# Projections of keys, queries and values into pairs of PSUM banks, with the convolution over all 1024 tokens at once

## The chip, the cores and the metric

The kernel runs on one core of a Trainium2 chip. The metric is the device time of one launch in microseconds (us). TensorE does the matmuls, VectorE (DVE in the profile), ScalarE (ACT) and GpSimd (POOL) the work on elements, and SyncE's queue (SP) issues the transfers. TensorE writes its results into PSUM, which has eight banks of 512 float32 values in each of 128 partitions.

## The reference

One decoder layer on 1024 tokens of width 1024: a half-step SwiGLU network, a mixer with two branches (gated delta rule and sparse attention), and a second half-step network. What matters here is the first branch's input:

```python
proj = h @ w_in[l]
(dn_qkv, dn_z, dn_b, dn_a, c_q, c_kv, idx_k_raw, idx_w,
 gate_a, gate_b) = split_cols(proj, IN_SPLITS)
qkv = jax.nn.silu(causal_dwconv(dn_qkv, conv_w[l])).astype(jnp.float32)
dq, dk_, dvv = split_cols(qkv, (DN_QK_W, DN_QK_W, DN_V_W))
```

The convolution is causal, has four taps, and treats each of the 3072 channels by itself: eight heads of 128 channels for each of queries, keys and values, so 24 times 128 channels.

## The kernel before, in words

Activations lie with channels on the partitions and tokens along the free dimension, in two halves of 512 tokens. Every float32 product is made of three matmuls (`mm3`, lines 139 to 141): each operand is split into a high part and a low part (`split`, lines 111 and 112: ScalarE copies the high part, VectorE or GpSimd subtracts it).

The stages, with their place in the profiled execution: the first feed-forward network (to 689 us), small projections and index queries (`small_proj`, `index_queries`, to 815), index scores (`scores`, to 904), the heads' projections and convolutions (`kq_head` for keys and queries, `v_head` for values, to about 1230), the joining of the solved triangular blocks with the gates' projections (`solve_join`, to 1315), the delta rule (`delta`, to 1600), attention (`attn_head`, to 1853), the output projection (`out_proj`, matmuls into `pwo`, from 1818 on) and the second feed-forward network.

PSUM is one pool for the whole program. Each stage builds a `Banks` object over it, which gives names to banks: a tile with tag `g` takes banks 0 and 1 in turn, `u` banks 2 and 3, `t` and `d` banks 4 to 7. `gemm` projects 1024 tokens onto 128 channels: 24 matmuls for each half into one bank called `pin`. The convolution (`conv`, lines 950 to 963) then works on each half: ScalarE copies the half with the fourth tap's weight (line 957), VectorE adds the other three taps out of PSUM (line 960, 511 to 509 elements), for the second half three more instructions add the one to three tokens that reach over from the first (line 962), and ScalarE applies Silu (line 963).

The order of instructions on each engine is found by a scheduler from the order of the program, its priorities and the tiles' dependencies; a later stage's instructions may be placed among an earlier one's where their tiles are free. Lines marked with `keep_in_program_order` are not moved.

The names that the steps below touch: `n_acc` and `n_ps` are a norm's sums of squares (GpSimd, then a matmul with ones, line 204), `rs_y` its inverse root on VectorE (lines 101 to 106), `n_rb` that root spread over the partitions by matmuls (line 181). `kq` and `vT` are convolved keys and queries, and values. `pq` are index queries, `arg` the exponents of the decays (line 920), `tb` an activation of the gates (line 1161), `sp_r` a latent being normalised (line 696). In the delta rule `o` is a head's output and `pot` its transposition. In attention `pl` are logits, `ph` and `plo` split probabilities, `pp` their transposition, and `pao` their product with the values; `mh` and `ml` are the split merged branches that `out_proj` reads.

Of the kernel before, what the change touches and what calls it, by code (L numbers as in the profile page):

```python
# [10 lines left out]
F32 = mybir.dt.float32  # L11
# [46 lines left out]
class Banks:  # L58
# [5 lines left out]
    def tile(self, shape, dtype, name, tag):  # L64
# [2 lines left out]
        self.turn[tag] += 1  # L67
        return self.pool.tile(shape, dtype, name=name, tag=f"bank{i}", bufs=1)


class Layer:
    def __init__(self, ctx, tc, I, out):
        self.ctx, self.tc, self.nc, self.I, self.out = ctx, tc, tc.nc, I, out
        self.pinned = False
        nc = self.nc
        self.const = self.pool(ctx, "const", 1)
        self.dram = ctx.enter_context(tc.tile_pool(name="dram", bufs=1, space=DRAM))
        self.stat = self.pool(ctx, "stat", 2)
        self.wp = self.pool(ctx, "w", 1)
        self.psum = self.pool(ctx, "psum", 1, space=PSUM)  # L80
        self.ident = self.const.tile([P, P], F32, name="ident")
        make_identity(nc, self.ident)
        self.ones = self.const.tile([P, P], F32, name="ones")
        nc.vector.memset(self.ones, 1.0)
# [83 lines left out]
    def pair(self, j, h):  # L168
        return self.part(j, h, 0), self.part(j, h, 1)
# [549 lines left out]
    def index_queries(self, tmp, ps, cqr, fill):  # L719

        nc = self.nc
        wh, wl = self.weights([self.I["w_iq"][0].rearrange("(k p) f -> p k f", p=P)], 2, 512)
        qs = tmp.tile([P, NB_IDX, 768], F32R, name="qs")
        for t0, n in ((256, 256), (512, 512)):
            for c in range(4):
                pq = ps.tile([P, 512], F32, name="pq", tag="g" if c % 2 else "u")
                for k in range(2):
                    self.mm3(pq[:, 0:n], wh[:, k, ts(c, P)], wl[:, k, ts(c, P)], cqr[0][:, k, t0:t0 + n],
                             cqr[1][:, k, t0:t0 + n], k == 0, k == 1)
                o = slice(t0 - 256, t0 - 256 + n)  # L730
# [205 lines left out]
        w = self.I["w_in"][0].rearrange("(k p) f -> p k f", p=P)  # L936
        return self.weights([w[:, :, c:c + m] for c, m in zip(cols, widths)], NK, sum(widths), self.splitter)

    def gemm(self, ps, weights, tags, halves=range(2)):

        wh, wl = weights
        n = wh.shape[-1]
        out = []
        for h in halves:
            pp = ps.tile([P, 512], F32, name="pin", tag=tags[h])
            for k in range(NK):
                self.mm3(pp[0:n], wh[:, k, :], wl[:, k, :], self.hhi[k][h], self.hlo[k][h], k == 0, k == NK - 1)
            out.append(pp)
        return out

    def conv(self, p, tile_i, pps, dest):

        nc = self.nc
        cw = self.cw.rearrange("p (j c) -> p c j", j=4)[:, tile_i, :]
        for h in range(2):
            y = p.tile([P, 512], F32, name="cv_y", tag="cv_y", bufs=3)
            nc.scalar.activation(y, pps[h], AF.Copy, scale=cw[:, 3:4])
            for j in (2, 1, 0):
                n = 3 - j
                nc.vector.scalar_tensor_tensor(y[:, n:512], pps[h][:, 0:512 - n], cw[:, j:j + 1], y[:, n:512], ALU.mult, ALU.add)  # L960
                if h:
                    nc.vector.scalar_tensor_tensor(y[:, 0:n], pps[0][:, 512 - n:512], cw[:, j:j + 1], y[:, 0:n], ALU.mult, ALU.add)
            nc.scalar.activation(dest(h), y, AF.Silu)

    def kq_head(self, hd, p, ps, picks):
        nc = self.nc
        kq = p.tile([P, 2, S], F32, name="kq", tag="kq", bufs=1)
        pk = self.gemm(ps, self.columns((1024 + hd * P,)), "gu")
        self.conv(p, 8 + hd, pk, lambda h: kq[:, 0, ts(h, 512)])
        pq = self.gemm(ps, self.columns((hd * P,)), "gu")  # L970
        picks(2)
        self.conv(p, hd, pq, lambda h: kq[:, 1, ts(h, 512)])

        ss = self.stat.tile([P, 2, NT], F32, name="ss")
        kts = []
        for h in range(2):
            for i in range(2):
                pt = ps.tile([P, 512], F32, name="pt", tag="t")
                for t in range(4):
                    nc.tensor.transpose(pt[:, ts(t, P)], kq[:, i, ts(4 * h + t, P)], self.ident)  # L980
                j = p.tile([P, 512], F32, name="qk_j", tag="qk_j", bufs=1)
# [28 lines left out]
        for h in range(2):  # L1010
            pg = ps.tile([P, 4, P], F32, name="pgram", tag="t")
            for t in range(4):
                for i in range(2):
                    c = 8 * h + 2 * t + i
# [17 lines left out]
    def v_head(self, hd, p, ps):  # L1032

        nc = self.nc
        pv = self.gemm(ps, self.columns((2048 + hd * P,)), "gu")
        vT = p.tile([P, S], F32, name="vT", tag="vT", bufs=1)
        self.conv(p, 16 + hd, pv, lambda h: vT[:, ts(h, 512)])
        for h in range(2):
            pt = ps.tile([P, 4, P], F32, name="pt", tag="t")
            for t in range(4):  # L1040
                nc.tensor.transpose(pt[:, t, :], vT[:, ts(4 * h + t, P)], self.ident)
            vb = p.tile([P, 4, P], F32, name="vb", tag="vb", bufs=2)
            nc.vector.tensor_mul(vb, pt, self.beta[:, hd, ts(h, 4), None].to_broadcast([P, 4, P]))
            nc.sync.dma_start(self.vbd[ts(h, 4), :, hd, :].rearrange("t p d -> p t d"), vb)
# [435 lines left out]
    def run(self):  # L1480
        nc, tc, I = self.nc, self.tc, self.I
# [8 lines left out]
        hs = ExitStack()  # L1490
        self.open_parts(hs, "hT", 0, NK, "right")
        with ExitStack() as c:
            ps = Banks(self.psum, s=(0, 1, 2, 3, 4, 5), m=(6, 7))
            self.open_x(c)
            np_ = self.pool(c, "norm1", 1)
            self.open_parts(c, "rest1", NK, 14)
# [31 lines left out]
            self.down_last(I["ffn1_wd"], 2 * NS, np_, ps, keep_x, to_mix)  # L1528
        merged, ms = self.mixer(hs)
        with ExitStack() as c:  # L1530
            ps = Banks(self.psum, s=(0, 1, 2, 3, 4, 5), m=(6, 7))
            self.open_x(c)
            self.new_x(load=True)
            np_ = self.pool(c, "norm2", 1)
# [29 lines left out]
    def mixer(self, hs):  # L1564

        nc = self.nc
        ms = ExitStack()
        with ExitStack() as km:
            keep = self.pool(km, "keep", 1)
            self.masks(keep)  # L1570
            with ExitStack() as ss:
                ps = Banks(self.psum, g=(0, 1), u=(2, 3), t=(4, 5, 6, 7), d=(4, 5, 6, 7))
                gpool = self.pool(ss, "gates", 1)
                gates = self.gates(gpool)
                self.gate_ps, self.splitter = ps, "gpsimd"
# [26 lines left out]
                with ExitStack() as c2:  # L1602
                    sp = self.pool(c2, "blocks", 1)
                    blocks = [self.solve_blocks(k, sp, ps) for k in range(2)]
                    with ExitStack() as c3:
                        p = self.pool(c3, "qkv", 1)
# [23 lines left out]
                    fill(2)  # L1630
                    fill(2)
                self.delta_state(keep)
                ps = Banks(self.psum, g=(0,), u=(2,), pq=(4, 5), pv=(1, 3), pn=(6, 7), po=(1, 3), qk=(0, 2))
                self.gate_ps, self.splitter = ps, "vector"
                dpool = self.pool(ss, "delta", 1)
                first = self.attn_first((gpool, "tz", 2), ps)
# [9 lines left out]
                for _ in first:  # L1646
                    pass
            with ExitStack() as c:
                ps = Banks(self.psum, qk=(0, 1), lg=(2, 4, 5), pt=(6, 7), ao=(3,))
                p = self.pool(c, "attn", 1)  # L1650
                mlp = self.pool(c, "merged_raw", 1)
                raw = [mlp.tile([P, S], F32, name=f"mr{k}", tag=f"mr{k}") for k in range(NK)]
# [75 lines left out]
```

## Time and profile before

| | us |
|---|---|
| median of 3 runs (lowest, highest) | 2591.26 (2591.16, 2594.76) |
| profiled execution, its own time | 2597.29 |
| its span (first to last instruction) | 2595.6 |
| TensorE busy | 2515.3 |
| VectorE busy | 1723.2 |
| ScalarE busy | 1186.2 |
| GpSimd busy | 931.1 |

The mean granted clock of TensorE is 0.981 of full speed. All durations below come from the profiled execution, which is 6.0 us longer than the median of the runs. A row of a timeline gives the start, the duration, the engine, the line, the tiles (out<-in) and, in brackets, how long the engine idled before it and for whom. The duration of a matmul reaches into the next one, so their pace is read from the starts.

### The profile page before, as it was taken

The page shows a single profiled execution, that of the slowest core. Times are in us where ns is not written, and L with a number is a line of the kernel's source. Part 1 is how long each engine was busy: PE and PEld are TensorE (multiplying, and loading weights), DVE is VectorE, ACT ScalarE, POOL GpSimd, SP SyncE. Part 2 cuts the span into 40 slices and gives each one's busy share as a digit, 9 for nine tenths or more (in the row PEclk, how much of TensorE's full clock was granted, in tenths as well). Part 3 has the DMA queues.
Part 4 walks back from the last instruction along what each step waited for, and adds up shares of the span by engine and source line. Part 5 has one row for each costly group of instructions (what it writes and reads, how often), then busy time and mean ns, then how long its engine had stood idle before and what let it go on. Part 6 is the DMA issues. An engine that isn't in the chain of part 4 may idle for free.

```text
span 2595.6 us, 36363 instructions
## 1 busy us (share of the span) xinstructions
PE 2515.3 (97%) x12694; PEld 2068.8 (80%) x12694; DVE 1723.2 (66%) x3419; ACT 1186.2 (46%) x2314; POOL 931.1 (36%) x721
## 2 busy tenths in 40 slices
PE   7999999999999989989999999999999999999998
PEld 6788888888787778867778887998787888888886
DVE  6755566676555677899746685777667555557766
ACT  4444344333434566546258636655434444444333
POOL 1555445333434223332200002443325554554340
PEclk9999999999999989999999899999999999999999
DMA  6243345962435144544553323222541434439642
GB/s 192 91 150 132 111 142 171 325 219 86 142 87 138 57 116 124 136 111 125 139 201 99 118 94 96 82 74 76 189 132 57 142 102 146 138 128 322 226 144 74
DMA packets 364376, 352.73 MB, mean 136 GB/s; under 512 B 87128, under 2 KB 271264, under 8 KB 363168
## 3 DMA queue, kind: packets, MB, share of 16 engines
q1 hardware_dynamic: 354848, 332.05, 40.1%
q10 hardware_dynamic: 8064, 16.78, 1.8%
q0 software_dynamic: 1280, 1.57, 0.3%
q8 instruction: 100, 1.64, 0.3%
q14 instruction: 84, 0.69, 0.1%
HBM read 234.35 MB, written 115.98 MB: 135 GB/s over the span
## 4 chain that ended last, share of the span: by engine, by line
PE 50%; DVE 7%; ACT 1%; issue 1%; DMA 0%; DVEq 0%; ACTq 0%
PE pst L139 8%; PE pst L141 8%; PE pst L140 8%; PE pin L141 2%; PE pin L139 2%; PE pin L140 2%; DVE sb_p L1071 2%; PE pn L1258 1%; PE po L1267 1%; PE pv L1253 1%; DVE cv_y L960 1%; PE pq L1248 1%; PE pwo L140 1%; PE pwo L139 1%; PE pwo L141 1%; PE pp L1372 1%
## 5 line engine op out<-in xcount | busy, mean ns | idle before, releaser
L139 PE MATMUL pst<-p,w_hi 128*128 128x512 f32 x960 | 377.9, 394 | 1.4 <-ACT p L257 0.9
L141 PE MATMUL pst<-p,w_hi 128*128 128x512 f32 x960 | 376.2, 392 | 1.8 <-DVE w_hi L112 1.8
L140 PE MATMUL pst<-p,w_hi 128*128 128x512 f32 x960 | 375.6, 391 | 1.3 <-DVE p L112 1.3
L139 PE MATMUL pin<-p,w_hi 128*128 128x512 f32 (+1 forms) x848 | 342.5, 405 | 6.4 <-DVE cv_y L960 4.2
L140 PE MATMUL pin<-p,w_hi 128*128 128x512 f32 (+1 forms) x848 | 341.0, 402 | 0.5 <-DVE p L112 0.5
L141 PE MATMUL pin<-p,w_lo 128*128 128x512 f32 (+1 forms) x848 | 340.8, 402 | 0.0
L111 ACT CAST w_hi<-w_raw 128x512 fp32r<-128x512 f32 (+2 forms) x282 | 196.3, 699 | 300.9 <-PE pst L141 126.8
L112 DVE TENSOR_TENSOR w_lo<-w_raw,w_lo 128x512 fp32r<-128x512 f32 (+1 forms) x196 | 191.5, 978 | 163.7 <-ACT w_lo L111 162.2
L141 PE MATMUL pst<-p,w_lo 128*128 128x512 f32 x728 | 284.6, 391 | 0.0
L140 PE MATMUL pst<-p,w_lo 128*128 128x512 f32 x728 | 284.4, 391 | 0.0
L139 PE MATMUL pst<-p,w_lo 128*128 128x512 f32 x728 | 282.7, 393 | 0.0
L141 PEld LDWEIGHTS pst<-p,w_hi 128*128 128x128 f32 x960 | 180.8, 188 | 43.0 <-DVE w_hi L112 2.4
L139 PEld LDWEIGHTS pst<-p,w_hi 128*128 128x128 f32 x960 | 181.0, 189 | 41.5 <-ACT p L257 1.3
L140 PEld LDWEIGHTS pst<-p,w_hi 128*128 128x128 f32 x960 | 180.8, 188 | 40.8 <-DVE p L112 1.7
L111 ACT CAST w_lo<-w_raw 128x512 fp32r<-128x512 f32 (+1 forms) x196 | 113.1, 580 | 199.0 <-DMA w_raw<-in_ffn_wg_dram 83.1
L139 PEld LDWEIGHTS pin<-p,w_hi 128*128 128x128 f32 (+1 forms) x848 | 162.0, 191 | 43.3 <-DVE cv_y L960 4.5
L141 PEld LDWEIGHTS pin<-p,w_lo 128*128 128x128 f32 (+1 forms) x848 | 161.9, 191 | 37.0 <-issue 3.1
L140 PEld LDWEIGHTS pin<-p,w_hi 128*128 128x128 f32 (+1 forms) x848 | 162.1, 191 | 36.4 <-issue 2.6
L411 DVE TENSOR_TENSOR c<-c,pst 128x512 f32<-128x512 f32 x120 | 82.0, 683 | 151.8 <-PE pst L141 113.7
L112 POOL TENSOR_TENSOR w_lo<-w_raw,w_hi 128x1024 fp32r<-128x1024 f32 (+1 forms) x43 | 106.7, 2482 | 199.6 <-ACT w_hi L111 173.2
L141 PEld LDWEIGHTS pst<-p,w_lo 128*128 128x128 f32 x728 | 136.7, 188 | 30.8
L139 PEld LDWEIGHTS pst<-p,w_lo 128*128 128x128 f32 x728 | 136.7, 188 | 30.1 <-ACT c L375 0.6
(432 smaller groups left out, 5461.7 us busy)
## 6 DMA issues: line engine op xcount, KB each, us to landing
p<-mixd SPq DMA_DIRECT2D x144, 256.0 KB, 5.6
w_raw<-in_w_in_dram SPq DMA_DIRECT2D x52, 512.0 KB, 4.0
w_raw<-in_ffn_wg_dram SPq DMA_DIRECT2D x44, 512.0 KB, 3.8
w_raw<-in_ffn_wu_dram SPq DMA_DIRECT2D x44, 512.0 KB, 3.9
mixd<-t_hi SPq DMA_DIRECT2D x72, 256.0 KB, 4.4
mixd<-t SPq DMA_DIRECT2D x72, 256.0 KB, 4.0
w_raw<-in_ffn_wd_dram SPq DMA_DIRECT2D x48, 384.0 KB, 4.3
actd<-c SPq DMA_DIRECT2D x70, 256.0 KB, 2.0
```

The source lines that it names most:

```text
L111: self.nc.scalar.copy(hi, raw)
L112: self.pin((self.nc.vector if engine == "vector" else self.nc.gpsimd).tensor_sub(lo, raw, hi))
L139: mm(ps, lhsT=wh, rhs=rh, start=first, stop=False, **kw)
L140: mm(ps, lhsT=wh, rhs=rl, start=False, stop=False, **kw)
L141: mm(ps, lhsT=wl, rhs=rh, start=False, stop=last, **kw)
L411: nc.vector.tensor_add(c[i, h], c[i, h], bank["y" if m == 1 else "z"])
L960: nc.vector.scalar_tensor_tensor(y[:, n:512], pps[h][:, 0:512 - n], cw[:, j:j + 1], y[:, n:512], ALU.mult, ALU.add)
L1071: nc.vector.tensor_mul(v, T[:, 0:i, 0:i].rearrange("p j c -> p c j"), L[:, None, 0:i, i].to_broadcast([P, i, i]))
L1248: nc.tensor.matmul(pq[:, i, :], lhsT=kq[:, h, ts(c, P)], rhs=old[:, h, :], start=True, stop=True)
L1253: nc.tensor.matmul(pv[r, i, :], lhsT=X[r, h, :], rhs=vb[r, h, :], start=True, stop=True)
L1258: nc.tensor.matmul(pn[:, i, :], lhsT=kd[r, h, :], rhs=vn[r, h, :], start=True, stop=True)
L1267: nc.tensor.matmul(po[r, i, :], lhsT=at[r, h, :], rhs=vn[r, h, :], start=True, stop=True)
```

## The change

`gemm` and `index_queries` take a tile of two banks side by side, called a pair, where they took two tiles of one bank; banks 0 to 3 become two pairs. The convolution reads a pair as 1024 tokens in a row: one copy, three instructions of VectorE and one Silu. Its buffer `cv_y` holds 1024 tokens and exists twice, where there were three of 512. The one PSUM pool is replaced by a pool for each stage, opened and closed with it: one for each feed-forward network, one for the mixer up to the join, one for the delta rule, one for attention.

```diff
+    def pair(self, name, tag="w"):
+        pairs = self.names[tag]
+        i = pairs[self.turn[tag] % len(pairs)]
+        self.turn[tag] += 1
+        return self.pool.tile([P, 2, 512], F32, name=name, tag=f"pair{i}", bufs=1)
...
-        self.psum = self.pool(ctx, "psum", 1, space=PSUM)
...
             for c in range(4):
-                pq = ps.tile([P, 512], F32, name="pq", tag="g" if c % 2 else "u")
+                if c % 2 == 0:
+                    both = ps.pair("pq")
+                pq = both[:, c % 2]
...
-    def gemm(self, ps, weights, tags, halves=range(2)):
+    def gemm(self, ps, weights, tags, halves=range(2), whole=False):
...
+        both = ps.pair("pin") if "w" in ps.names else None
         for h in halves:
-            pp = ps.tile([P, 512], F32, name="pin", tag=tags[h])
+            pp = both[:, h] if both is not None else ps.tile([P, 512], F32, name="pin", tag=tags[h])
...
-        return out
+        return both.rearrange("p h t -> p (h t)") if whole else out
...
-        for h in range(2):
-            y = p.tile([P, 512], F32, name="cv_y", tag="cv_y", bufs=3)
-            nc.scalar.activation(y, pps[h], AF.Copy, scale=cw[:, 3:4])
-            for j in (2, 1, 0):
-                n = 3 - j
-                nc.vector.scalar_tensor_tensor(y[:, n:512], pps[h][:, 0:512 - n], cw[:, j:j + 1], y[:, n:512], ALU.mult, ALU.add)
-                if h:
-                    nc.vector.scalar_tensor_tensor(y[:, 0:n], pps[0][:, 512 - n:512], cw[:, j:j + 1], y[:, 0:n], ALU.mult, ALU.add)
-            nc.scalar.activation(dest(h), y, AF.Silu)
+        y = p.tile([P, S], F32, name="cv_y", tag="cv_y", bufs=2)
+        nc.scalar.activation(y, pp, AF.Copy, scale=cw[:, 3:4])
+        for j in (2, 1, 0):
+            n = 3 - j
+            nc.vector.scalar_tensor_tensor(y[:, n:S], pp[:, 0:S - n], cw[:, j:j + 1], y[:, n:S], ALU.mult, ALU.add)
+        nc.scalar.activation(dest, y, AF.Silu)
...
-            ps = Banks(self.psum, s=(0, 1, 2, 3, 4, 5), m=(6, 7))
+            ps = Banks(self.pool(c, "psum", 1, space=PSUM), s=(0, 1, 2, 3, 4, 5), m=(6, 7))
...
-                ps = Banks(self.psum, g=(0, 1), u=(2, 3), t=(4, 5, 6, 7), d=(4, 5, 6, 7))
+                pp = ExitStack()
+                ps = Banks(self.pool(pp, "psum", 1, space=PSUM), w=(0, 1), t=(4, 5, 6, 7), d=(4, 5, 6, 7))
...
-                ps = Banks(self.psum, g=(0,), u=(2,), pq=(4, 5), pv=(1, 3), pn=(6, 7), po=(1, 3), qk=(0, 2))
+                pp.close()
+                ps = Banks(self.pool(ss, "psum", 1, space=PSUM), g=(0,), u=(2,), pq=(4, 5), pv=(1, 3), pn=(6, 7), po=(1, 3), qk=(0, 2))
...
-                ps = Banks(self.psum, qk=(0, 1), lg=(2, 4, 5), pt=(6, 7), ao=(3,))
+                ps = Banks(self.pool(c, "psum", 1, space=PSUM), qk=(0, 1), lg=(2, 4, 5), pt=(6, 7), ao=(3,))
```

The scheduler moves instructions in consequence. First, TensorE between the first network and the mixer: `n_ps` and `n_rb` belong to the norm of the second half of the tokens, `p0_00` to `p7_01` are the first half's activations (high and low), `p0_10` and on the second half's. Before:

```order
L139 MATMUL pin_6169<-p7_00_5535,w_hi_6165 128x512
L140 MATMUL pin_6169<-p7_01_5536,w_hi_6165 128x512
L141 MATMUL pin_6169<-p7_00_5535,w_lo_6166 128x512
L181 MATMUL n_rb_5806<-ident_69,rs_y_5793 128x128 x4
L139 MATMUL pin_5923<-p0_10_5509,w_hi_5894 88x512
L139 MATMUL pin_6134<-p0_10_5509,w_hi_6105 128x512
L140 MATMUL pin_5923<-p0_11_5510,w_hi_5894 88x512
L141 MATMUL pin_5923<-p0_10_5509,w_lo_5895 88x512
```

and with the change:

```order
L210 MATMUL n_ps_5782<-ones_71,n_acc_5612 128x1
L210 MATMUL n_ps_5782<-ones_71,n_sq_5779 128x1
L187 MATMUL n_rb_5806<-ident_66,rs_y_5793 128x128 x4
L145 MATMUL pin_5902<-p0_00_5507,w_hi_5898 88x512
L146 MATMUL pin_5902<-p0_01_5508,w_hi_5898 88x512
L147 MATMUL pin_5902<-p0_00_5507,w_lo_5899 88x512
L145 MATMUL pin_5902<-p1_00_5511,w_hi_5898 88x512
L146 MATMUL pin_5902<-p1_01_5512,w_hi_5898 88x512
```

Before, projections of the first half (72 matmuls into three `pin`) stand ahead of `n_rb` and the second half's behind it. Now the norm's `n_ps` and `n_rb` follow the last down-projection with nothing between, and the first projection, `pin_5902`, comes behind them, first half and then second.

Second, TensorE at the end of attention: `pao_17261` and `pao_17012` are the last head's product with the values, `n_rb` spreads its normaliser. Before:

```order
L141 MATMUL pwo_17493<-mh6_17330,w_lo_17490 128x512
L139 MATMUL pwo_17493<-mh7_17331,w_hi_17489 128x512
L140 MATMUL pwo_17493<-ml7_17339,w_hi_17489 128x512
L141 MATMUL pwo_17493<-mh7_17331,w_lo_17490 128x512
L140 MATMUL pao_17261<-plo_17297,vh_16569 128x256
L141 MATMUL pao_17261<-ph_17296,vl_16573 128x256
L139 MATMUL pao_17261<-ph_17296,vh_16569 128x128
L140 MATMUL pao_17261<-plo_17297,vh_16569 128x128
L141 MATMUL pao_17261<-ph_17296,vl_16573 128x128
L181 MATMUL n_rb_17312<-ident_69,a_r_17307 128x128 x4
L139 MATMUL pwo_17565<-mh0_17324,w_hi_17561 128x512
```

and with the change:

```order
L147 MATMUL pao_17012<-ph_17047,vl_16324 128x256
L145 MATMUL pao_17012<-ph_17047,vh_16320 128x128
L146 MATMUL pao_17012<-plo_17048,vh_16320 128x128
L147 MATMUL pao_17012<-ph_17047,vl_16324 128x128
L187 MATMUL n_rb_17063<-ident_66,a_r_17058 128x128 x4
L145 MATMUL pwo_17177<-mh0_17075,w_hi_17173 128x512
L146 MATMUL pwo_17177<-ml0_17083,w_hi_17173 128x512
L147 MATMUL pwo_17177<-mh0_17075,w_lo_17174 128x512
L145 MATMUL pwo_17177<-mh1_17076,w_hi_17173 128x512
```

Before, output projections (`pwo`) stand among the last heads' instructions and on both sides of `n_rb`; there are 72 ahead of it. Now none stands ahead of it, and all 384 follow.

Third, VectorE in one convolution, of the second head's keys. Before:

```order
L960 SCALAR_TENSOR_TENSOR cv_y_7842<-pin_7792,cw_3807,cv_y_7842 128x511
L960 SCALAR_TENSOR_TENSOR cv_y_7842<-pin_7792,cw_3807,cv_y_7842 128x510
L960 SCALAR_TENSOR_TENSOR cv_y_7848<-pin_7817,cw_3807,cv_y_7848 128x511
L960 SCALAR_TENSOR_TENSOR cv_y_7842<-pin_7792,cw_3807,cv_y_7842 128x509
L962 SCALAR_TENSOR_TENSOR cv_y_7848<-pin_7792,cw_3807,cv_y_7848 128x1
L960 SCALAR_TENSOR_TENSOR cv_y_7848<-pin_7817,cw_3807,cv_y_7848 128x510
L962 SCALAR_TENSOR_TENSOR cv_y_7848<-pin_7792,cw_3807,cv_y_7848 128x2
L960 SCALAR_TENSOR_TENSOR cv_y_7848<-pin_7817,cw_3807,cv_y_7848 128x509
L962 SCALAR_TENSOR_TENSOR cv_y_7848<-pin_7792,cw_3807,cv_y_7848 128x3
```

and with the change, with what follows:

```order
L968 SCALAR_TENSOR_TENSOR cv_y_7810<-pin_7761,cw_3807,cv_y_7810 128x1023
L968 SCALAR_TENSOR_TENSOR cv_y_7810<-pin_7761,cw_3807,cv_y_7810 128x1022
L968 SCALAR_TENSOR_TENSOR cv_y_7810<-pin_7761,cw_3807,cv_y_7810 128x1021
L821 TENSOR_SCALAR pk_cand_7591<-pk_m_7590 128x6
L822 TENSOR_TENSOR pk_thr_7595<-pk_cand_7591,pk_flip_7592 128x6
```

Nine instructions on two tiles of 512 tokens (`cv_y_7842` and `cv_y_7848`) became three on one of 1024, and the next instructions, those that pick the largest scores, stand behind the three.

## Rows read from the trace of the kernel before

**Rows 1.** the page: TensorE's busy us, share of the span, instructions.

```profile
PE 2515.3 (97%) x12694; PEld 2068.8 (80%) x12694; DVE 1723.2 (66%) x3419; ACT 1186.2 (46%) x2314; POOL 931.1 (36%) x721
```

**Rows 2.** stretch, us: busy PE, PEld, DVE, ACT, POOL; clock, DMA share, GB/s.

```profile
1100.00:1190.00 90.00, 78.88 (x400) 62.41 (x399) 88.91 (x184) 46.85 (x82) 32.91 (x18) 0.94 0.45 121
```

**Rows 3.** TensorE's waits, 895 to 1240 us: in total, times, longest.

```profile
PE pt L980 <- ACT kq L963: 16.6, 3, 12.5
PE pin L139 <- DVE cv_y L960: 4.2, 1, 4.2
PE pt L1041 <- ACT vT L963: 2.1, 2, 1.9
```

**Rows 4.** `pin` matmuls by stretch; TensorE's timeline (start, duration) between them.

```profile
689.20:699.50 10.30, 10.14 (x43) 7.12 (x43) 0.00 (x0) 0.00 (x0) 1.00 0.48 145
701.20:708.40 7.20, 6.90 (x29) 5.23 (x29) 0.00 (x0) 1.67 (x3) 1.00 0.07 20
709.50:715.20 5.70, 3.67 (x15) 2.54 (x16) 0.00 (x0) 0.24 (x1) 1.00 0.00 0
689.05 0.39 PE L141 MATMUL pd<-p,w_lo 128*128 128x512 f32 x1
699.52 0.28 PE L204 MATMUL n_ps<-ones,n_acc 128*128 128x1 f32 x2
708.46 1.05 PE L181 MATMUL n_rb<-ident,rs_y 128*128 128x128 f32 x8
```

**Rows 5.** timelines of GpSimd and VectorE in the same place.

```profile
694.92 1.29 POOL L194 TENSOR_TENSOR n_acc<-n_acc,n_sq 128x512 f32<-128x512 f32 x1
701.40 0.16 DVE L206 TENSOR_SCALAR n_a<-n_ps 128x4 f32<-128x4 f32 x1 [7.60 <-PE n_ps L204]
704.36 0.15 DVE L106 SCALAR_TENSOR_TENSOR rs_y<-rs_t,rs_y 128x4 f32<-128x4 f32 x1
```

**Rows 6.** VectorE by shape: busy us, mean ns; line 962: min/median/max ns.

```profile
L960 DVE SCALAR_TENSOR_TENSOR cv_y<-pin,cw,cv_y 128x511 f32<-128x511 f32 x48 | 35.7, 745 | 17.7 <-ACT cv_y L957 17.6
L962 DVE SCALAR_TENSOR_TENSOR cv_y<-pin,cw,cv_y x72: 197/208/223, 914.4 to 1227.1; 128x1 f32<-128x1 f32 x24, 128x2 f32<-128x2 f32 x24, 128x3 f32<-128x3 f32 x24
L112 DVE TENSOR_TENSOR w_lo<-w_raw,w_hi 128x1024 fp32r<-128x1024 f32 x27 | 34.8, 1291 | 38.9 <-ACT w_hi L111 22.0 <-DMA odd<-w_lo 15.3 <-PE pq L1248 1.4
```

**Rows 7.** TensorE's timeline (starts first) behind its wait of 4.2 us.

```profile
1147.01 0.63 PE L141 MATMUL pin<-p,w_lo 128*128 128x512 f32 x1
1147.44 0.63 PE L139 MATMUL pin<-p,w_hi 128*128 128x512 f32 x1
1151.71 0.39 PE L140 MATMUL pin<-p,w_hi 128*128 128x512 f32 x1
1151.94 0.39 PE L141 MATMUL pin<-p,w_lo 128*128 128x512 f32 x1
```

**Rows 8.** `pwo` matmuls by stretch; VectorE's and TensorE's timeline there.

```profile
1818.00:1844.40 26.40, 14.30 (x48) 9.54 (x48) 0.00 (x0) 0.87 0.20 61
1844.40:1853.10 8.70, 5.92 (x25) 4.37 (x24) 0.00 (x0) 1.00 0.42 121
1823.64 8.12 DVE L112 TENSOR_TENSOR ml<-mr,mh 128x512 fp32r<-128x512 f32 x8
1831.68 1.27 DVE L1376 TENSOR_TENSOR plo<-pp,ph 128x512 fp32r<-128x512 f32 x2
1832.41 0.39 PE L140 MATMUL pao<-plo,vh 128*128 128x256 f32 x1 [2.04 <-DVE plo L1376]
```

**Rows 9.** TensorE's waits, 765 to 816 us.

```profile
PE pq L139 <- ACT tb L1161: 3.8, 2, 2.3
PE n_rb L181 <- DVE sp_r L696: 2.6, 1, 2.6
```

**Rows 10.** timeline of TensorE at the end of the delta rule.

```profile
1598.85 2.38 PE L1227 MATMUL pot<-ident,o 128*128 128x128 f32 x8 [2.07 <-ACT o L1222]
1602.35 0.47 PE L139 MATMUL pl<-p,p 128*128 128x128 f32 x1 [1.12 <-ACT w_lo L1228]
```

More of the change, by code (lines that the diff above doesn't have):

```diff
@@ L948, in gemm, with conv @@
             out.append(pp)
-        return out
-    def conv(self, p, tile_i, pps, dest):
+        return both.rearrange("p h t -> p (h t)") if whole else out
+    def conv(self, p, tile_i, pp, dest):
         nc = self.nc
         cw = self.cw.rearrange("p (j c) -> p c j", j=4)[:, tile_i, :]
-        for h in range(2):
-            y = p.tile([P, 512], F32, name="cv_y", tag="cv_y", bufs=3)
-            nc.scalar.activation(y, pps[h], AF.Copy, scale=cw[:, 3:4])
-            for j in (2, 1, 0):
-                n = 3 - j
-                nc.vector.scalar_tensor_tensor(y[:, n:512], pps[h][:, 0:512 - n], cw[:, j:j + 1], y[:, n:512], ALU.mult, ALU.add)
-                if h:
-                    nc.vector.scalar_tensor_tensor(y[:, 0:n], pps[0][:, 512 - n:512], cw[:, j:j + 1], y[:, 0:n], ALU.mult, ALU.add)
-            nc.scalar.activation(dest(h), y, AF.Silu)
+        y = p.tile([P, S], F32, name="cv_y", tag="cv_y", bufs=2)
[4 more added lines that the diff above has]
+        nc.scalar.activation(dest, y, AF.Silu)
     def kq_head(self, hd, p, ps, picks):
@@ L967, in kq_head @@
         kq = p.tile([P, 2, S], F32, name="kq", tag="kq", bufs=1)
-        pk = self.gemm(ps, self.columns((1024 + hd * P,)), "gu")
-        self.conv(p, 8 + hd, pk, lambda h: kq[:, 0, ts(h, 512)])
-        pq = self.gemm(ps, self.columns((hd * P,)), "gu")
+        pk = self.gemm(ps, self.columns((1024 + hd * P,)), "gu", whole=True)
+        self.conv(p, 8 + hd, pk, kq[:, 0])
+        pq = self.gemm(ps, self.columns((hd * P,)), "gu", whole=True)
         picks(2)
-        self.conv(p, hd, pq, lambda h: kq[:, 1, ts(h, 512)])
+        self.conv(p, hd, pq, kq[:, 1])
         ss = self.stat.tile([P, 2, NT], F32, name="ss")
@@ L1034, in v_head @@
         nc = self.nc
-        pv = self.gemm(ps, self.columns((2048 + hd * P,)), "gu")
+        pv = self.gemm(ps, self.columns((2048 + hd * P,)), "gu", whole=True)
         vT = p.tile([P, S], F32, name="vT", tag="vT", bufs=1)
-        self.conv(p, 16 + hd, pv, lambda h: vT[:, ts(h, 512)])
+        self.conv(p, 16 + hd, pv, vT)
         for h in range(2):
@@ L1530, in run @@
         with ExitStack() as c:
-            ps = Banks(self.psum, s=(0, 1, 2, 3, 4, 5), m=(6, 7))
+            ps = Banks(self.pool(c, "psum", 1, space=PSUM), s=(0, 1, 2, 3, 4, 5), m=(6, 7))
             self.open_x(c)
```

## The prediction

> **What bounds the kernel now.** I read the page first: TensorE is busy for 97% of the span [rows 1]. The change issues the same matmuls and weight loads as before, so it can only win or lose time in which TensorE idles or runs slowly: 2595.6 − 2515.3 = 80 us of idling, and the stretches behind long gaps. Next I read the table by stretches for 1100 to 1190 us, where heads are projected and convolved: VectorE is busy for 88.91 of 90 us, TensorE for 78.88 [rows 2]. There VectorE sets the pace, and the convolution is VectorE work. Then the waits of TensorE from 895 to 1240 us [rows 3]: 16.6 us for a finished convolution of keys or queries, of which one wait of 12.5 lies at the first head, and some 6 for values and for a bank that a convolution still reads. Last I read, in timelines, the places where the stages join, since the change also closes one PSUM pool and opens another there.
>
> [...]
>
> **The change part by part.** + means slower.
>
> *The convolution on VectorE.* Before, it takes six instructions of 0.745 us and three of 0.208 [rows 6]: 5.1 us. Now it takes three over 1021 to 1023 elements. No row shows that shape; the nearest is VectorE's subtraction over 1024, 1.291 us, so 3.8 us, and 1.3 us saved. The bounds are no saving beyond the small instructions (0.6 us) and a slope by width alone (1.4). There are 24 convolutions, so about 30 us of VectorE; ScalarE's two copies and two Silus become one each, and that is costed at nothing because VectorE, not ScalarE, is full here. [...]
>
> *What this gives on TensorE (term C).* Of the waits in [rows 3] all but the first head's 12.5 can shrink: 16.6 + 4.2 + 2.1 − 12.5, with smaller ones some 11 us, plus 2.6 for the slow stretch behind each of two long ones: 16 at most. The first head's wait ends with VectorE's backlog of index scores and stays. About ten convolutions fall into 1100 to 1190 us, 13 us of VectorE. Against it, a convolution now starts only when both halves are projected, the two banks come free together, and Silu waits for all. I take half: **−8** (0 to −16).
>
> *End of the first feed-forward network (term A).* Before, behind the last down-projection, TensorE runs projections of the first token half while the second half's norm is made: 43 of them in 10.3 us, 29 in the next 7.2, 15 in the 5.7 after [rows 4], 87 by 715.2. Their banks were free ones of the one pool. Now the order on TensorE has the norm's sums (n_ps) and its spread (n_rb) ahead of all of them. n_ps needs GpSimd's last sum, 694.92 + 1.29 = 696.2 [rows 5]; GpSimd's order is as before. So TensorE idles from 689.4 (689.05 + 0.39) to 696.2, does n_ps in 1.9 (699.52 to 701.40), idles through VectorE's root (701.40 to 704.51, 3.1), and does n_rb (half of 1.05), to 701.8. The 24 projections of the first half follow, thirteen at 0.43 us and eleven at 0.23, to 710; the second half's 24 at 0.23 end at 715.5, if their splits come in time. That makes 48 done where before had 87: 39 × 0.23 = 9.0. **+9** (5 to 11).
>
> *Index queries (term B).* Later, before loses 3.8 us to an activation of the gates and 2.6 to VectorE ahead of n_rb [rows 9]. These waits end with other engines, so part of A's lateness disappears in them, and the gates' projections no longer stand where they hold a query's bank. But VectorE now has all eight exponent blocks (`arg`) ahead of the latents' norm. **−3** (−8 to +6).
>
> *End of attention (term D).* Before, TensorE fills the last head's waits with output projections: 48 from 1818 to 1844.4 us, 25 (one on the edge) to 1853.1 [rows 8], 72 in all. Now all 384 stand behind the last n_rb of attention. VectorE's eight splits of 8.12 us from 1823.64 still stand ahead of the two `plo` that attention waits for (1831.68), so TensorE idles for about ten microseconds up to 1832.4. Without the 22 or so output projections that before stood between there and the end, the chain ends some 8.7 us sooner, near 1844.4. From there 8.7 / 0.23 = 38 fit before 1853.1, against 72 done: 34 × 0.23 = 7.8. The last network is bound by TensorE, so it stays. **+8** (5 to 10.5, with a slow stretch).
>
> *Delta rule to attention (term E).* Six small matmuls of logits (`pl`) filled the wait of 2.07 us ahead of `pot`; now they stand behind, 6 × 0.23 = 1.4, and the wait of 1.12 behind it [rows 10] stays. **+1.5** (0 to 3). Nothing else moves past SyncE's or GpSimd's queues, and no DMA is added: costed at nothing. If a weight load came late, it would show as TensorE waiting for `w_hi`.
>
> The sum is 9 − 3 − 8 + 8 + 1.5 = +7.5 on the profiled execution's 2597.3, that is 2604.8. That execution is 6.0 above the median of the runs, 2591.26, so on their scale **2598.8**. The three runs before spread over 0.14%; I call 0.2%, 5.2 us, what can be told from no change: 2586.1 to 2596.4.
>
> **The rivals.**
>
> *VectorE's saving comes out whole (faster).* It is the pace-maker of 1100 to 1190 us [rows 2], so its 30 us could take away all waits and slow stretches there, −16, with some 3 of the first head's, while the index queries take up the most, −8: 9 + 7.8 + 1.5 − 19 − 8 = −8.7, so 2582.6. It decides from where C and B together exceed 23.5. Against it: TensorE has hardly 16 us to give there.
>
> *It cancels (no change to tell).* C at −12 and D at 6 give 9 − 3 − 12 + 6 + 1.5 = +1.5, so 2592.8. For it: every term of the joints has some slack that the trace cannot show.
>
> *The larger grain makes new waits (much slower).* Two pairs stand where four banks stood, and a pair is free only after the third long instruction. Before, the first half's bank came free some 2.5 us sooner (two instructions of 1.29 [rows 6]). At five waits per stage like those of [rows 3] that is +12 against C = −8: 2598.8 + 12 = 2610.8. It decides if TensorE's next projection regularly finds its pair taken. [...]
>
> *The change does not do what it says:* the order of instructions shows it in both respects, so I give it no chance.
>
> **How the numbers follow.** Forecast 0.44, cancels 0.22, saving whole 0.19, new waits 0.15. Slower by over 0.2%: 0.44 + 0.15 = 0.59; within 0.22; faster 0.19. The range goes from just above the faster rival, 2584, to just above the slowest, 2612; about 2 in 10 lie outside.
>
> **What would show it.** Right: 7 us of idling ahead of n_ps and 3 ahead of n_rb near 690 to 702 us, then slow starts; an idle stretch near 10 us ahead of `plo` in attention's tail; VectorE's convolution at about 1.27 us per instruction; the wait of 4.2 for a bank gone or shorter. Wrong: projections still running during the last norm; a convolution instruction near 1.49; new waits of projections on convolutions between 920 and 1060 us, where TensorE is dense now.

## The result, and the profile after

The changed kernel takes 2636.62 us (median of four runs, 2631.36 to 2638.36) against 2592.62 (2591.16 to 2594.76) for the kernel before: a ratio of 1.0164, with a 95% interval of 1.0146 to 1.0182. That is 44.0 us slower by the medians (42.5 by the ratio), well outside the predicted range of 2584 to 2612. The profiled execution took 2638.12 us. Of all runs in this document one, of e7, was disturbed (3159.06 us) and is left out of its median and ratio.

The page first, the line that answers to [rows 1]:

```profile
span 2636.4 us, 36141 instructions
PE 2519.7 (96%) x12694; PEld 2067.6 (78%) x12694; DVE 1700.3 (64%) x3275; ACT 1181.2 (45%) x2266; POOL 930.5 (35%) x721
```

TensorE does the same 12694 matmuls, in 4.4 us more. Its idling went from 80.3 us (2595.6 − 2515.3) to 116.7 (2636.4 − 2519.7): +36.4. The two together are the 40.8 us by which the spans differ. VectorE was busy for 22.9 us less, and what that gave was outweighed. The waits of TensorE over the whole span (in total, times, longest) say where:

```profile
PE pv L1259 <- ACT tb L1167: 16.1, 1, 16.1
PE pin L145 <- DVE pk_inc L828: 12.6, 1, 12.6
...
PE pao L146 <- DVE plo L1382: 8.1, 9, 4.0
PE n_ps L210 <- POOL n_acc L200: 6.7, 1, 6.7
PE pao L145 <- ACT osa L1387: 5.1, 1, 5.1
PE pin L145 <- DVE cv_y L968: 4.8, 2, 3.8
...
PE pq L145 <- DVE lo L743: 4.2, 3, 2.3
```

The first row is new and the largest: one wait of 16 us of the delta rule's first matmul (`pv`) for an activation of the gates (`tb`). The second is the wait of 12.5 at the first head [rows 3]; now a projection (`pin`) waits there, before it was a transposition (`pt`). `n_ps`, `plo` and `osa` are the joints of the stages. By place (span less busy TensorE, from the table by stretches with its bounds laid at the same instructions of both kernels), idling in us:

| place | before | after |
|---|---|---|
| end of the first network (term A) | 2.0 | 9.2 |
| index queries (B) | 7.4 | 8.4 |
| first head's wait | 12.5 | 12.7 |
| heads and convolutions (C) | 11.1 | 9.9 |
| joining of the blocks | 4.2 | 6.2 |
| **from there into the delta rule** | 0 | 16.2 |
| delta rule to attention (E) | | −0.3 |
| attention's tail (D) | 4.8 | 13.4 |

(E is a difference; the delta rule itself adds 1.4, small places the rest.) Next the rows that answer to [rows 2] and to the predicted steps. By stretch: us, busy PE, PEld, DVE, ACT, POOL, clock, DMA share, GB/s; the second is the new wait:

```profile
1100.00:1210.00 110.00, 100.40 (x504) 80.23 (x503) 104.41 (x193) 56.18 (x87) 37.33 (x20) 0.97 0.46 125
1316.00:1336.00 20.00, 3.85 (x18) 3.14 (x17) 5.57 (x19) 10.77 (x19) 0.00 (x0) 0.63 0.90 328
```

VectorE is still full where heads are convolved (104.41 of 110 us): it has less to do for each head, and does other work instead. In the second stretch no engine on elements is full, but the DMA engines are busy at 0.90. TensorE's timeline at the joints, against [rows 4] and [rows 8]:

```profile
695.16 0.59 PE L210 MATMUL n_ps<-ones,n_acc 128*128 128x1 f32 x2 [6.69 <-POOL n_acc L200]
...
701.25 2.04 PE L187 MATMUL n_rb<-ident,rs_y 128*128 128x128 f32 x8 [2.52 <-DVE rs_y L112]
...
1334.17 3.67 PE L1259 MATMUL pv<-vb,X 64*64 64x128 f32 x16 [16.15 <-ACT tb L1167]
...
1857.71 0.58 PE L145 MATMUL pao<-ph,vh 128*128 128x256 f32 x1 [5.11 <-ACT osa L1387]
1863.62 0.58 PE L146 MATMUL pao<-plo,vh 128*128 128x256 f32 x1 [4.05 <-DVE plo L1382]
...
1876.45 0.47 PE L145 MATMUL pwo<-mh,w_hi 128*128 128x512 f32 x1
```

The idling ahead of `n_ps` and `n_rb` is there as worked out (6.8 and 3.1 were forecast), and the first output projection (`pwo`) starts at 1876.45, where before 72 were done by the end of attention. Last the projections (`pin`) in the stretch of [rows 4]; 46 of them ran by 715.2 (48 were forecast, 87 before), at a granted clock of 0.74:

```profile
689.20:715.20 26.00, 12.25 (x46) 8.16 (x47) 0.00 (x0) 0.00 (x0) 0.74 0.23 66
```

### The profile page after: what moved, and what is told of

It reads as the page before. It is cut to its first block, busy times and chain, and to the rows that moved or that the text cites. A ratio compares the mean times of both kernels' runs of the same rounds, so it can differ in the third digit from the quotient of the medians.

```text
span 2636.4 us, 36141 instructions
## 1 busy us (share of the span) xinstructions
PE 2519.7 (96%) x12694; PEld 2067.6 (78%) x12694; DVE 1700.3 (64%) x3275; ACT 1181.2 (45%) x2266; POOL 930.5 (35%) x721
## 3 DMA queue, kind: packets, MB, share of 16 engines
q8 instruction: 100, 1.64, 0.3%
## 4 chain that ended last, share of the span: by engine, by line
PE 55%; DVE 9%; DMA 2%; ACT 1%; issue 1%; POOL 0%; DVEq 0%; ACTq 0%; SPq 0%
PE pst L145 7%; PE pst L147 7%; PE pst L146 7%; PE pin L145 4%; PE pin L146 4%; PE pin L147 4%; DVE sb_p L1077 2%; DVE cv_y L968 1%; PE pv L1259 1%; PE po L1273 1%; PE pn L1264 1%; PE pq L1254 1%; PE pwo L147 1%; PE pwo L146 1%; PE pwo L145 1%
## 5 line engine op out<-in xcount | busy, mean ns | idle before, releaser
L145 PE MATMUL pin<-p,w_hi 128*128 128x512 f32 (+1 forms) x848 | 344.2, 406 | 24.5 <-DVE pk_inc L828 12.6
```

The lines of the kernel that those rows point to most:

```text
L145: mm(ps, lhsT=wh, rhs=rh, start=first, stop=False, **kw)
```

## The experiments

Two theories stood first, numbered in the expectations: that the pools do nearly all of it, and that the pairs, released as a whole, do a large part. Runs of one batch share the runs of the kernel before. Its median changed by batch (2589.86 to 2594.43), so ratios are compared, or runs of the same batch.

| run | median us | ratio to before [95%] |
|---|---|---|
| changed kernel | 2636.62 | 1.0164 [1.0146, 1.0182] |
| e1, pools only | 2614.82 | 1.0098 [1.0082, 1.0115] |
| e2, late pool | 2629.97 | 1.0156 [1.0139, 1.0174] |
| e3, two pools | 2627.24 | 1.0142 [1.0122, 1.0163] |
| e5, convolution in halves | 2648.93 | 1.0232 [1.0212, 1.0253] |
| e6, picks later | 2637.36 | 1.0159 [1.0142, 1.0176] |
| e7, three pairs | 2627.69 | 1.0134 [1.0116, 1.0151] |
| e8 = e2 + e6 | 2628.51 | 1.0130 [1.0115, 1.0145] |
| e9, second buffer | 2613.24 | 1.0096 [1.0082, 1.0110] |
| e10, before + second buffer | 2591.99 | 1.0009 [0.9997, 1.0020] |
| e11 = e2 + second buffer | 2606.45 | 1.0067 [1.0053, 1.0081] |
| e12 = e3 + second buffer | 2606.68 | 1.0050 [1.0036, 1.0065] |
| e13 = e1 + second buffer | 2608.38 | 1.0049 [1.0034, 1.0064] |

### The parts of the change: e1 and e5

e1 is the kernel before with the pools of the change alone; banks and convolution stay as they were.

```diff
-        self.psum = self.pool(ctx, "psum", 1, space=PSUM)
...
-                ps = Banks(self.psum, g=(0, 1), u=(2, 3), t=(4, 5, 6, 7), d=(4, 5, 6, 7))
+                pp = ExitStack()
+                ps = Banks(self.pool(pp, "psum", 1, space=PSUM), g=(0, 1), u=(2, 3), t=(4, 5, 6, 7), d=(4, 5, 6, 7))
...
-                ps = Banks(self.psum, g=(0,), u=(2,), pq=(4, 5), pv=(1, 3), pn=(6, 7), po=(1, 3), qk=(0, 2))
+                pp.close()
+                ps = Banks(self.pool(ss, "psum", 1, space=PSUM), g=(0,), u=(2,), pq=(4, 5), pv=(1, 3), pn=(6, 7), po=(1, 3), qk=(0, 2))
```

> The kernel before with only the PSUM pools split by stage; tiles stay single banks and the convolution stays in halves. Theory 1 (the joints of the stages cost, whatever the form of the tiles): TensorE idles about 9 us ahead of n_ps and n_rb, 8 to 9 us more in attention's tail, and at the start of the delta rule it waits for a late activation of the gates (10 to 18 us, by pv or by the first pn); the time is 2622 to 2637. Theory 2 (the pair is what costs, because two halves come free together): the first two stay, but no wait over 3 us stands at the start of the delta rule, and the time is 2604 to 2614.

e5 is the changed kernel with the convolution in halves again, reading the pair.

```diff
-        y = p.tile([P, S], F32, name="cv_y", tag="cv_y", bufs=2)
-        nc.scalar.activation(y, pp, AF.Copy, scale=cw[:, 3:4])
...
+        pps = [pp[:, ts(h, 512)] for h in range(2)]
+        for h in range(2):
+            y = p.tile([P, 512], F32, name="cv_y", tag="cv_y", bufs=3)
+            nc.scalar.activation(y, pps[h], AF.Copy, scale=cw[:, 3:4])
...
```

> The changed kernel with the convolution of the kernel before, half by half, reading the two halves of a pair. Theory 1 (the whole convolution gains almost nothing, since TensorE's waits in that stage are bank and order waits that stay): 2634 to 2641. Rival (the whole convolution's shorter VectorE time is a gain that the joints hide): over 2643, with TensorE's waits between 1100 and 1240 us grown by 6 us or more.

The pools alone cost 23.7 us (2614.82 − 2591.08, the same batch): more than half of the loss, but not nearly all. That is just above the 2604 to 2614 of theory 2, and clearly under the 2622 of theory 1, which fell. At the entry of the delta rule e1 waits little, if more than the 3 us that theory 2 allowed (waits, 1300 to 1340 us):

```profile
PE pn L1257 <- ACT vn L1253: 3.8, 1, 3.8
PE pv L1252 <- issue: 0.8, 1, 0.8
```

Its waits in the convolution stage are those of [rows 3], to the tenth. So the pairs do the rest: e5 is 34.1 us slower than e1 (same batch). It has the same wait of `pv` for `tb` (15.6), and these between 895 and 1260 us:

```profile
PE pin L145 <- DVE cv_y L972: 21.6, 5, 9.5
PE pt L990 <- ACT kq L973: 11.0, 1, 11.0
```

Before, projections waited 4.2 us for a bank that VectorE still read, once; with pairs released as a whole 21.6, five times. That is the rival "larger grain" in its place. Other waits became shorter; in all, TensorE waits 35 us from 895 to 1240 us in e5 and 24 in e1. The whole convolution takes this back (22.5 us in the changed kernel), as e5's rival had it: e5 takes over 2643 us, and its waits from 1100 to 1240 us are 19.1 us against 9.5. The changed kernel is 12.3 us faster than e5 by medians of two batches, 10.5 by spans (2646.9 − 2636.4), 17.6 by the ratios. So **the idea does work**, and is outweighed: +23.7 (pools) + 34.1 (pairs) − 12.3 (whole convolution) = +45.5, the distance of 2636.62 from this batch's 2591.08; by the ratios +0.98% + 1.34% − 0.68% = +1.64%.

### The pools: e2 and e3

e2 lets the delta rule, attention and the second network share one pool:

```diff
+                self.late = self.pool(self.ctx, "psum", 1, space=PSUM)
-                ps = Banks(self.pool(ss, "psum", 1, space=PSUM), g=(0,), u=(2,), ...
+                ps = Banks(self.late, g=(0,), u=(2,), ...
...
-                ps = Banks(self.pool(c, "psum", 1, space=PSUM), qk=(0, 1), lg=(2, 4, 5), pt=(6, 7), ao=(3,))
+                ps = Banks(self.late, qk=(0, 1), lg=(2, 4, 5), pt=(6, 7), ao=(3,))
```

> The changed kernel, but delta rule, attention and second network share one PSUM pool. Theory 1: output projections stand among attention's last instructions again, the tail's idling falls from 13 to about 5 us, the wait of 16 us at the start of the delta rule stays; 2625 to 2630. Rival (the tail's idling comes from late operands, not from the pool): nothing changes, 2633 to 2638.

e3 lets, beside that, the first network share a pool with the mixer; its banks 0 to 3 are then halves of the pairs.

```diff
+        if self.halves and i < 4:
+            if i % 2 == 0:
+                self.both = self.pool.tile([P, 2, 512], F32, name=name, tag=f"pair{i // 2}", bufs=1)
+            return self.both[:, i % 2]
...
-                ps = Banks(self.pool(pp, "psum", 1, space=PSUM), w=(0, 1), t=(4, 5, 6, 7), d=(4, 5, 6, 7))
+                ps = Banks(self.first, w=(0, 1), t=(4, 5, 6, 7), d=(4, 5, 6, 7))
```

> As the run with the late pool, and the first network shares a pool with the mixer's first part: the network's banks 0 to 3 are halves of the pairs. Theory 1: 48 projections stand ahead of the norm's n_rb again, the two idle stretches of 6.7 and 2.5 us fall to 2 to 4 in all; the first bank of the delta rule is one that no gate holds, so the wait of 16 us moves to the second pv or shrinks; 2605 to 2622. Rival (pairs as banks of the network make TensorE wait there): idling before 690 us grows by more than 5 us and the time is over 2625.

In e2 output projections stand among attention's matmuls again, and the tail's waits (1815 to 1880 us) are

```profile
PE pao L147 <- DVE plo L1383: 2.9, 3, 2.0
PE pwo L147 <- DVE ml L119: 1.3, 2, 0.7
...
```

where the changed kernel has 6.7 for `plo` and 5.1 for `osa` (1840 to 1880 us). The tail's idling falls from 13.4 to about 5 us. The time is read best from two pairs of runs of one batch each, below: e8 is 8.9 us under e6, e11 6.8 under e9. That is term D, forecast at +8, with E, since delta rule and attention share the pool too. By its own ratio e2 can't be told from the changed kernel (1.0156 and 1.0164); its span is 10.6 us shorter (2636.4 − 2625.8).

In e3 48 projections fill the norm at the end of the first network again, and its waits for `n_ps` and `n_rb` are gone. But the first network itself now waits for banks (waits, 85 to 705 us):

```profile
PE pd L151 <- DVE x L512: 1.7, 1, 1.7
PE pst L151 <- DVE x L512: 1.6, 1, 1.6
PE pin L151 <- ACT w_hi L123: 1.6, 1, 1.6
PE pd L151 <- DVE x L554: 1.0, 1, 1.0
PE pst L153 <- DVE w_hi L124: 0.7, 1, 0.7
```

The kernel before, which has one pool too but single banks, waits there once, for 1.8 us and for a load. Both halves of a pair are one tile of the program, free only when both have been read. These five waits come to 6.6 us, against the 9.2 (6.69 and 2.52) that are gone at the joint, and so most of what the joint gave was lost in the stage: 2627.24 against e2's 2629.97, within what the two vary by. It lies above the 2605 to 2622 expected here. At the start of the delta rule `pv` still waits 8.9 us for `tb` and then 4.7 for its load.

### The wait of 16 us: e6, e7, e8, e9

ScalarE's timeline in the changed kernel:

```profile
1318.94 0.60 ACT L1167 ACTIVATE tb<-pin 128x512 f32<-128x512 f32 x1
1323.32 0.33 ACTq L1168 DMA_DIRECT2D gbd<-tb  x1
1323.70 0.83 ACT L807 ACTIVATE pk_ja<-sc,pk_thr 128x640 f32<-128x640 f32 x1 [4.16 <-DMA vb<-vbd]
...
1332.40 1.15 ACT L807 ACTIVATE pk_ja<-sc,pk_thr 128x1024 f32<-128x1024 f32 x1
1333.45 0.19 ACT L807 ACTIVATION_READ_ACCUMULATOR pk_ja<-sc,pk_thr 128x1 f32 x1
1333.55 0.58 ACT L1167 ACTIVATE tb<-pin 128x512 f32<-128x512 f32 x1
```

The last gates' projection lies in a pair. Each half is read by one `tb`, and both must be done before any bank of that pair, and with it the bank of `pv`, is free (the second `tb` ends at 1334.13, and `pv` starts at 1334.17). Between the two `tb` stand eight counts of the sparse selection (`pk_ja`, 1323.70 to 1333.64). My theory was that the second `tb` is queued behind these counts. The rival: the tile `tb` exists once, so its second writer waits for the store of the first (`gbd`). e6 moves the counts to a later step of the delta rule:

```diff
-                    picks(2)
+                    if i > 1:
+                        picks(2)
```

> The changed kernel; the picking of the largest scores starts two steps of the delta rule later, so that on ScalarE the gates' last activations stand ahead of it. If the wait of 16 us at the start of the delta rule is for an activation that is queued behind eight counts on ScalarE: the wait goes, a wait of 3 to 5 us for the first loads of the delta rule takes its place, and the time is 2619 to 2627. If the wait comes from the closing of the pool itself, pv still waits over 10 us and the time is 2632 to 2640.

```profile
1321.15 0.60 ACT L1167 ACTIVATE tb<-pin 128x512 f32<-128x512 f32 x1
1324.27 0.33 ACTq L1168 DMA_DIRECT2D gbd<-tb  x1
1332.26 0.60 ACT L1167 ACTIVATE tb<-pin 128x512 f32<-128x512 f32 x1 [10.51 <-DMA gbd<-tb]
```

The counts are gone from this place, ScalarE idles for 10.51 us, and `tb` still starts 11 us after its twin: `pv` waits 12.7 instead of 16.1, and the time is that of the changed kernel (1.0159 and 1.0164). My theory fell: without the counts the store holds `tb` nearly as long. e8 is the same on e2, and `pv` waits 12.6:

> The run with the late pool and the picking two steps later together. If the joints' costs add up: 2629.97 less 9 to 14, so 2616 to 2621, still slower than before by some 25 us. If the wait at the start of the delta rule and the tail hide one another: 2624 to 2630.

It took 2628.51 us: e6 had given nothing that could be added.

e7 has three pairs instead of two, and two banks instead of four for the rest:

```diff
-                ps = Banks(self.pool(pp, "psum", 1, space=PSUM), w=(0, 1), t=(4, 5, 6, 7), d=(4, 5, 6, 7))
+                ps = Banks(self.pool(pp, "psum", 1, space=PSUM), w=(0, 1, 2), t=(6, 7), d=(6, 7))
```

> The changed kernel with three pairs and two single banks in the mixer's first part, where it has two pairs and four. If the pairs' waits come from their number: TensorE's waits for convolutions (some 8.6 us) and for index queries (7 us) fall by half or more and the time is 2618 to 2630. Rival: two single banks are too few for transposes and blocks, new waits of pt, pgram or pd take their place, and the time is 2640 or more.

Its three runs lie between 2627.32 and 2632.45. The wait of `pv` is gone, the index queries' waits for `lo` fall from 7.0 to 3.3 us, and none is left for `cv_y`, as expected if the number of pairs matters. But with two banks the stage waits elsewhere. From 895 to 1300 us:

```profile
PE pin L145 <- DVE pk_pos L814: 9.4, 1, 9.4
PE pd L758 <- ACT relu L761: 8.4, 27, 0.8
PE pt L986 <- ACT qk_j L988: 2.5, 1, 2.5
PE pt L986 <- DVE vb L1049: 2.2, 1, 2.2
```

The index scores (`pd`) wait 27 times for 8.4 us, the transpositions in many small waits. Three pairs and two banks are all eight that the kernel divides. e9 gives `tb` two buffers, the ones of its neighbour `tz`, and changes no PSUM:

```diff
-                tb = p.tile([P, 512], F32, name="tb", tag="ta", bufs=1)
+                tb = p.tile([P, 512], F32, name="tb", tag="tz", bufs=2)
```

> The changed kernel; the gates' last activation (tb) goes to the two buffers of tz where it had the one of ta, so the second half needn't wait for the first half's store. If the pair at the start of the delta rule is held by that chain (activation, store, activation): the wait of 16 us falls to what the first loads leave, 2 to 6 us, and the time to 2620 to 2627. If something else holds the bank, pv waits over 10 us and the time stays at 2632 to 2640.

ScalarE and TensorE in e9:

```profile
1320.40 1.09 ACT L1167 ACTIVATE tb<-pin 128x512 f32<-128x512 f32 x2
...
1325.42 1.93 PE L1259 MATMUL pv<-vb,X 64*64 64x128 f32 x16 [0.91 <-DMA vb<-vbd]
```

Both `tb` run back to back, `pv` starts 8.8 us sooner and waits for its load only. By stretch, 1318 to 1340 us, TensorE is busy for 19.38 us of 22 at a clock of 1.00:

```profile
1318.00:1340.00 22.00, 19.38 (x108) 15.50 (x107) 6.73 (x22) 14.03 (x26) 0.00 (x0) 1.00 0.76 283
```

The changed kernel has 5.85 us there, at a clock of 0.57. The spans differ by 21.1 us (2636.4 − 2615.3): 17.0 less idling, and 4.1 less time for the same matmuls. By the ratios the gain is 0.68%, 17.6 us, by medians of two batches 23.4. So one line, a second buffer in SBUF, took back two fifths to half of the loss, more than was expected. More came of it than the wait of 16 itself, since the matmuls behind this gap ran slower, as did those behind 4.2 us in [rows 7]: in the changed kernel `pv` takes 3.67 us where it takes 1.93 here, and nine projections behind it start every 0.43 us instead of 0.23, some 3.6 us in all.

### The second buffer on the others: e10 to e13

The same edit of one line as in e9, on the kernel before, on e2, on e3 and on e1.

> The kernel before with the same two buffers for tb. There the first bank of the delta rule is free, so nothing changes at that joint; the index queries' waits of 3.8 us for tb should go: 2585 to 2590 against 2592. If those waits have another cause (the queue of ScalarE): 2590 to 2595.

> The run with the late pool and the second buffer together. If the costs of the joints add up: 2630 less what the second buffer gives the changed kernel (10 to 16), so 2613 to 2620.

> The run with two pools and the second buffer together. If the first network's waits on pairs give back what the norm's joint gains, as in the run with two pools: 2601 to 2607, not below the 2606 of the late pool with the second buffer by more than 4. If the norm's joint is worth its full 9 us once nothing stands behind it: 2594 to 2600.

> The kernel before with split pools (single banks, halves) and the second buffer. If without pairs the chain of activation, store, activation costs only the wait of 3.8 us of pn: 2608 to 2613 against 2614.8. If it costs there as much as with pairs: 2592 to 2600.

e10 is no faster than before: the interval of its ratio holds 1, and the gain that I had expected is not there. In the kernel before, the store is as long (7.2 us to landing for both stores, of about 1301 and 1315), but `pv` takes a bank of its own and waits for nobody. The index queries still wait 3.2 us for `tb` in e10, against 3.8 [rows 9], so those waits have another cause, as the other branch (2590 to 2595) had it.

e11 is again better than expected, and e12 lies in the first of its ranges. The two come nearest for versions with pairs: 1.0067 and 1.0050, whose intervals overlap.

e13, with split pools but no pairs, is at 1.0049. Its time lies in the first range expected, but against e1 (1.0098) it gained 6.4 us by medians of two batches, 12.0 by spans (2614.3 − 2602.3) and some 13 by the ratios, whose intervals lie apart. The wait of `pn` (3.8) is only a part of it. Another part is the granted clock: of the 40 slices of the page, the one that holds the start of the delta rule is at 0.9 or more in e13 (1301 to 1366 us) and between 0.8 and 0.9 in e1 (1307 to 1372); what sets it is not shown. So the single buffer was harmless while one pool served the whole program (e10); it cost some 6 to 13 us once the pool was split, with single banks, and 18 to 23 with pairs.

With the second buffer in both, e9 (1.0096) and e13 (1.0049) differ by the pairs and the whole convolution alone. These two together still cost more than they give, some 12 us by the ratios (the intervals lie apart), 13.0 by spans (2615.3 − 2602.3; e13's profiled execution is the fastest of its six) and 4.9 by medians of two batches. Where, was not traced. No version is faster than the kernel before.

## Why the prediction was wrong

The direction was right, the size wrong (+7.5 forecast, about +43 measured, 40.8 by the profiled spans). By its steps:

**The sum has no term for the entry of the delta rule**: this is the step that failed. It rests on five places and closes with "Nothing else moves past SyncE's or GpSimd's queues, and no DMA is added: costed at nothing". The entry was put at nothing without a reason; before, TensorE waits for nobody there. It was a joint like A and D, and a pair stood across it. The rival "larger grain" had the mechanism, a pair free only after its last reader, but sought it between projections and convolutions, and priced five waits at +12. e5 shows that this cost exists where the convolution is in halves (`cv_y` 21.6 against 4.2). In the changed kernel it came as one wait of 16.15 us, whose last reader is not a convolution but an activation behind a store, with 4.1 us of slower matmuls. e6 and e9 show it. Of the 33 us between the forecast and the spans, some 20 lie here, 7 in term C and 4 in B.

**Term A**, +9: right. 6.69 and 2.52 us of idling, 46 projections by 715.2; the stage's idling grew by 7.2, and slow starts come on top. The slow stretch that the sum counts here and in term C, thirteen starts at 0.43 us instead of 0.23 or 2.6 us, is an estimate from [rows 7]; in the changed kernel nine projections behind `n_rb` start slowly (702.95 to 706.51 us). `n_ps` and `n_rb` themselves were priced too low (1.9 and 0.5 us; 3.6 and 1.7 from their first start to the end and to the next start, at a granted clock of 0.64 from 689 to 703 us).

**Term B**, −3: wrong in sign, +1. The gain that it named came with the pools alone: in e1 the index queries no longer wait for `tb` or `sp_r`, and from 690 to 870 us all that `pq` waits is

```profile
PE pq L138 <- DVE lo L734: 0.2, 1, 0.2
```

With pairs, a pair is held by VectorE's split of the queries (`lo`): 4.2 and 2.8 us of waiting. That is again the release of two banks at once.

**Term C**, −8: mis-sized; −1.2 of idling. The duration of the new instructions was forecast rightly. By shape (busy us, mean ns):

```profile
L968 DVE SCALAR_TENSOR_TENSOR cv_y<-pin,cw,cv_y 128x1023 f32<-128x1023 f32 x24 | 30.6, 1279 | 35.4 <-ACT cv_y L965 35.4
L968 DVE SCALAR_TENSOR_TENSOR cv_y<-pin,cw,cv_y 128x1022 f32<-128x1022 f32 x24 | 30.6, 1275 | 0.1
L968 DVE SCALAR_TENSOR_TENSOR cv_y<-pin,cw,cv_y 128x1021 f32<-128x1021 f32 x24 | 30.6, 1276 | 0.3
```

1.28 us each, as forecast from the subtraction of 1.291 [rows 6]. But the saving of 1.3 us in each convolution was worked out from durations, and the duration of a VectorE instruction reaches into the next one (by 0.07 to 0.10 us in the rows below), as that of a matmul does (0.63 us, with 0.43 between starts, in [rows 7]). Its timeline, three rows before and two after:

```profile
1167.36 0.74 DVE L960 SCALAR_TENSOR_TENSOR cv_y<-pin,cw,cv_y 128x511 f32<-128x511 f32 x1
1168.02 0.20 DVE L962 SCALAR_TENSOR_TENSOR cv_y<-pin,cw,cv_y 128x1 f32<-128x1 f32 x1
1168.15 0.15 DVE L814 TENSOR_TENSOR pk_thr<-pk_cand,pk_flip 128x6 int32<-128x6 int32 x1
...
1167.26 1.29 DVE L968 SCALAR_TENSOR_TENSOR cv_y<-pin,cw,cv_y 128x1023 f32<-128x1023 f32 x1
1168.45 1.04 DVE L1078 TENSOR_REDUCE sb_T<-sb_p 128x29 f32<-128x841 f32 x1
```

From start to start it is 0.66 us for 511 elements, 0.13 for one and 1.19 for 1023: 4.4 us for a convolution before, 3.6 after, 0.8 saved. The prediction should have gone by such starts, not by the durations. The time in which VectorE has a convolution running at all (the first number behind the length of the stretch, before and after) fell by 22.4 us, where 30 were forecast:

```profile
0.00:2595.00 2595.00, 114.07 (x216) 61.70 (x96) 0.98 0.43 136
0.00:2636.00 2636.00, 91.65 (x72) 51.68 (x48) 0.98 0.42 134
```

What failed besides is the half that I set against the gain: pairs took nearly all of it. e5 against the changed kernel gives the gain alone, 10 to 18 us by time and 12.6 of waits in this stage (35.1 − 22.5), about C's bound of 16; e5 against e1 gives its counterpart, 11.2 of waits (35.1 − 23.9).

**Term D**, +8: right, 8.6 of idling (e2 takes about 8 back). The waits came at `osa` and `plo`, where one wait of ten was forecast. **Term E**, +1.5: nothing (−0.3); small in either case.

Pools alone, A + D + E, were forecast at 18.5 (15.5 with B, whose reason lay in the pools too), and e1 gives 23.7 by medians, 18.7 by spans (2614.3 − 2595.6); the wait of `pn`, 3.8, is in no term. So the terms for the pools stood roughly, and what was missing was the entry of the delta rule, with a pair across it.

**The range** was made of errors in the places named, and the time left it through a place not looked at. The order of instructions had a part of it: in the change, eight `pk_ja` stand between the two `tb` on ScalarE, and `pv` behind both by its bank. To read off a released tile's last reader, its queue, its buffers and its store, at each place where a pool closes, was the step to add.

**Not settled:** why the store of `tb` is issued 3.8 us after its activation ends (1319.54 to 1323.32; in e9 the issue comes late too) was not tried; SyncE issues the delta rule's first loads in the same place, from 1315 to 1322 us. Nor were the 2 us at the joining of the blocks, all that e13 gains over e1, or where pairs and whole convolution still cost time with the second buffer.

## What to carry to other kernels

Two PSUM banks made into one tile came free together here, with the slowest reader of either half and whatever held that reader up: a tile in SBUF with one buffer, and behind it a store (16.15 us of waiting, gone with the second buffer in e9). Where tiles are joined to save instructions, follow each to its last reader at every place where the next stage takes its banks, and give that reader a second buffer first. A pool for each stage put the next stage's matmuls behind the last wait of the old one, 23.7 us in e1; idling grew where those had filled its waits (by 7.2 us in A and 8.6 in D). And what joining two instructions saves is read from the starts on the engine (0.8 us for a convolution), not from the durations (1.3).

## What was not expected

- A store of one `tb` (128 by 512 float32) held its buffer for 8.0 us from its issue (1324.27 to 1332.26 in e6), with the DMA engines busy at 0.95 there (1318 to 1336 us; 0.90 in the changed kernel from 1316 to 1336). In the changed kernel the median for these stores and their loads back is 2.7 us to landing, the longest 7.4.
- The convolution instructions of 1023 elements hold VectorE for 1.19 us each and those of 511 for 0.66: by estimate the part that does not grow with the width is about 0.13 us (2 × 0.66 − 1.19), where the durations make it 0.2 (2 × 0.745 − 1.279). The 22.4 us that the convolutions took less are nearly all of the 22.9 by which VectorE's busy time fell.
- An SBUF buffer that brings nothing before (e10, 1.0009) brings 18 to 23 us after the change.
